# Attention's values with two products per head instead of four, and the two parts summed afterwards

## The chip, the core and the metric

The kernel runs on one core of a Trainium2 chip. The core's engines work side by side, each through its own list of instructions in order: TensorE (PE: matrix products, with PEld for its weight loads), VectorE (DVE), ScalarE (ACT), GpSimd (POOL) and SyncE (SP, which issues transfers). They wait for each other through semaphores. The metric is the device time of one execution in microseconds (us); the median of several timed executions is given.

## What is computed

One decoder layer with 256 positions, 1024 channels and 8 heads of 64. With 256 positions there is one block of keys, so the attention is plain causal attention. Cut to what matters here:

```python
proj  = x @ w_in                     # q, k, v, and the inputs of the convolution and of the gates
p     = softmax(causal(q @ k.T) * scale)
y_att = (p @ v) @ w_attn_out         # the change is in p @ v, head by head
y_cnv = (B * causal_dwconv3(C * h)) @ w_conv_out
mix   = (sigmoid(g_att) * y_att + sigmoid(g_cnv) * y_cnv) @ w_o
x     = layer_norm(alpha * x + mix)
u     = causal_dwconv3(x @ w_up)
x     = layer_norm(alpha * x + (silu(u_gate) * u_val) @ w_down)
```

## The kernel before

**Two parts.** Every float32 operand of a product is split into a high part h (rounded to the type float32r) and a low part l = x - h. A product is the sum of h·h, h·l and l·h. For weights ACT makes h (tile `wh`, L212) and DVE makes l (tile `wl`, L222) from what the transfer brought (tile `raw`).

**Stages.** The products with `w_in` come first: q, k, v, then h, c, b of the convolution, then sixteen column blocks of the gates, g0 to g15. After them come y0 to y7 (the products with `w_attn_out` and `w_conv_out`), `w_o`, and the feed-forward part. Attention and convolution are worked out beside the gate products: DVE and ACT do their elementwise work while PE is on g0 to g15.

**Order.** The order on each engine is written out by hand. Work goes in slots, one for each unit of weights. The table `STEPS` says at which half slot each piece is issued on its engine: entry s is the first or second half of slot s // 2. An engine keeps that order; a piece that waits holds up all that stands behind it on the same engine.

**Attention's values.** Heads go in pairs p = 0 to 3, with j = 0, 1 inside a pair. `vpt` holds the values (`vp`: for each head, 64 columns of high parts and 64 of low parts) and the transposed probabilities (`PT`: a = 0 the high part, a = 1 the low part, made by L501 on ACT and L241 on DVE). `attend` forms the products (tile `av`), placed behind the products of slots 13, 19, 22 and 24: behind g1, g7, g10 and g12. In a result the first 64 rows come from the high parts of the values, the other 64 from the low parts. `attend_out` lets ACT copy the lower rows out of the bank (tile `ac`), `attend_sum` lets DVE add the upper rows, and `attend_h` and `attend_l` split the sum into the tile `aT`, which y0 to y7 read.

**Banks.** PSUM has eight banks of 512 columns. In this stage four (`acc_bank`) go round among g0 to g3, g6, g7 and g10 to g15, so that g15 takes the bank of g11 and g14 that of g10. The other four (`ps_bank`) serve the scores, the values (`av`), and g4, g5, g8 and g9. A gate block leaves its bank through two instructions: ACT copies one half out (tile `gs`, L847), then DVE adds the other half (L856, into the tile `gates`). Only then can the next owner of the bank begin on PE.

Of the kernel before, what the change touches and what calls it, by code (L numbers as in the profile page):

```python
# [13 lines left out]
AF = mybir.ActivationFunctionType  # L14
ALU = mybir.AluOpType

P = 128
S = 256
# [3 lines left out]
HD = 64  # L22
# [122 lines left out]
def layer_kernel(ctx: ExitStack, tc: tile.TileContext, x, wpack, cpack, ln1_g, ln1_b, ln2_g, ln2_b, out):  # L145
    nc = tc.nc
# [13 lines left out]
    def ps_bank(name):  # L160
        return ps_pool.tile([P, 512], F32, tag="ps", name=name)

    def scratch(shape, name, bufs=None, tag="scr"):
        return tmp.tile(shape, F32, tag=tag, name=name, bufs=bufs or 6)
# [75 lines left out]
    def low(l, src, h):  # L240
        nc.vector.tensor_tensor(l, src, h.bitcast(F32), op=ALU.subtract)  # L241
# [133 lines left out]
    vp = vpt[:, 0:2048].rearrange("p (t g n) -> p t g n", t=2, g=4)  # L375
    PT = vpt[:, 2048:3584].rearrange("p (a j n) -> p a j n", a=2, j=2)
    aT = yT = None
# [50 lines left out]
    SB, SM, PR = {}, {}, {}  # L428
# [77 lines left out]
    def attend(p):  # L506


        o = PR[p, "o"] = ps_bank(f"av{p}").rearrange("p (j s) -> p j s", j=2)
        for j in range(2):  # L510
            js = slice(j * P, (j + 1) * P)
            for a in range(2):
                nc.tensor.matmul(o[:, j], vp[:, 0, p, js], PT[:, a, j, 0:256], start=a == 0, stop=False)
            for a in range(2):
                nc.tensor.matmul(o[:, j, P:S], vp[:, 1, p, js], PT[:, a, j, 256:384], start=False, stop=a == 1)

    def attend_out(p):

        c = PR[p, "c"] = scratch([P, 2, S], f"ac{p}")
        nc.scalar.activation(c[0:HD], PR[p, "o"][HD:P], AF.Copy)  # L520

    def attend_sum(p):
        c, o = PR[p, "c"], PR[p, "o"]
        nc.vector.tensor_tensor(c[HD:P, 0], o[0:HD, 1], c[0:HD, 1], op=ALU.add)
        nc.vector.tensor_tensor(c[0:HD, 0], o[0:HD, 0], c[0:HD, 0], op=ALU.add)

    def attend_h(p):
        nonlocal aT
        if aT is None:
            aT = big.tile([P, 4, 2, S], F32R, tag="d8", name="aT")  # L530
        nc.scalar.activation(aT[:, p, 0, :], PR[p, "c"][:, 0], AF.Copy)

    def attend_l(p):
        low(aT[:, p, 1, :], PR[p, "c"][:, 0], aT[:, p, 0, :])

# [48 lines left out]
    def open_ps():  # L586
# [10 lines left out]
             s=[5, 11],  # L597
# [5 lines left out]
             h=[24, 30, 38, 44],  # L603
             l=[25, 36, 39, 45],
             av=[13, 19, 22, 24],
             out=[26, 39, 44, 49],
             sum=[35, 42, 49, 51],
             ah=[41, 47, 50, 54],
             al=[44, 52, 53, 55],
             c1=[21, 35],  # L610
# [35 lines left out]
    for p in range(4):  # L646
        on(1, STEPS["m"][p], masked, p)
        on(0, STEPS["e"][p], exps, p)
        on(1, STEPS["n"][p], normalize, p)
        on(1, STEPS["n"][p], probs_halves, p)  # L650
        on(1, STEPS["n"][p], probs_T, p)
        on(STEPS["wE"][p], STEPS["w"][p], probs_words, p)
        on(0, STEPS["h"][p], probs_h, p)
        on(1, STEPS["l"][p], probs_l, p)
        at(C0 + STEPS["av"][p], "pe", attend, p)
        on(0, STEPS["out"][p], attend_out, p)
        on(1, STEPS["sum"][p], attend_sum, p)
        on(0, STEPS["ah"][p], attend_h, p)
        on(1, STEPS["al"][p], attend_l, p)
# [542 lines left out]
    for k, (kind, i, u) in enumerate(seq[:tail_from]):  # L1202
        if kind == "u":
            c, v = i
# [143 lines left out]
```

## Time and profile before

| | |
|---|---|
| median of 3 timed executions | 357.79 us (357.71 to 358.07) |
| span of the profiled execution, first to last instruction | 355.8 us |
| timed median less that span | 2.0 us |
| PE busy | 348.1 us (98% of the span) |
| DVE busy | 302.0 us (85%) |
| ACT busy | 243.8 us (69%) |
| GpSimd busy | 15.5 us (4%) |

A busy time is the sum of what the engine's instructions took, without their overlaps. Products are pipelined, so that the distance between two starts, not the length of one, is what a product costs PE. The shares are averages over stages that differ.

### The profile page before, as it was taken

To read this page: it belongs to the slowest core of one execution; us is meant where nothing else is said; L and a number is where in the kernel's file an instruction comes from. 1 tells how busy PE (TensorE), PEld (TensorE's weight loads), DVE (VectorE), ACT (ScalarE), POOL (GpSimd) and SP (SyncE) were. 2 spreads that over 40 slices of the span, in tenths; PEclk is the share of its full clock that TensorE was granted. 3 is DMA by queue.
4 is the path that set the end of the run, shared out by engine and by line. 5 is a ranking of instruction groups with operands and counts; after the bars stand their busy time and mean duration, and the time that the engine had idled before them with its cause. 6 is when DMAs were issued, how large, how long until landed. Compare 5 with 4: busy or idle time off the path is not lost.

```text
span 355.8 us, 4907 instructions
## 1 busy us (share of the span) xinstructions
PE 348.1 (98%) x1739; PEld 294.6 (83%) x1739; DVE 302.0 (85%) x521; ACT 243.8 (69%) x391; POOL 15.5 (4%) x41
## 2 busy tenths in 40 slices
PE   9999999999999999999999999999999999999992
PEld 8888888888988888888888888888888888888881
DVE  4787787997999989989668969997998786999975
ACT  3767857889998976652557487794968576578800
POOL 2000000000000012410000000000000000000120
PEclk9999999999999999999999999999999999999998
DMA  7995986887575685689187775889769693833003
GB/s 244 428 395 204 232 280 236 151 256 206 130 255 186 204 331 202 204 304 354 30 206 236 238 192 222 243 243 341 188 268 251 239 291 125 281 131 121 0 0 119
DMA packets 44904, 77.99 MB, mean 219 GB/s; under 512 B 34896, under 2 KB 35536, under 8 KB 37840
## 3 DMA queue, kind: packets, MB, share of 16 engines
q1 hardware_dynamic: 44304, 75.59, 65.9%
q0 software_dynamic: 576, 2.10, 2.0%
q8 instruction: 13, 0.21, 0.3%
q14 instruction: 11, 0.09, 0.1%
HBM read 68.24 MB, written 1.05 MB: 195 GB/s over the span
## 4 chain that ended last, share of the span: by engine, by line
PE 95%; issue 2%; DVE 1%; POOLq 0%; POOL 0%; DVEq 0%
PE g L351 8%; PE u L333 8%; PE u L335 8%; PE u L334 8%; PE qk L692 6%; PE d L335 5%; PE d L333 5%; PE d L334 5%; PE g L358 4%; PE y L351 4%; PE pb L351 4%; PE v L692 3%; PE pb L358 2%; PE y L358 2%; PE o L335 2%; PE o L334 2%
## 5 line engine op out<-in xcount | busy, mean ns | idle before, releaser
L222 DVE TENSOR_TENSOR wl<-raw,wh 128x1024 fp32r<-128x1024 f32 x99 | 119.8, 1223 | 15.5 <-ACT wh L212 15.4
L212 ACT ACTIVATE wh<-raw 128x1024 fp32r<-128x1024 f32 x99 | 101.8, 1054 | 8.6 <-DMA raw<-in_wpack 8.6
L333 PE MATMUL u<-wh,x1T 128*128 128x512 f32 x128 | 49.8, 389 | 0.0
L334 PE MATMUL u<-wl,x1T 128*128 128x512 f32 x128 | 49.8, 389 | 0.0
L335 PE MATMUL u<-wh,x1T 128*128 128x512 f32 x128 | 49.8, 389 | 0.0
L351 PE MATMUL g<-xT,wh 128*128 128x512 f32 x128 | 31.2, 393 | 0.0
L333 PE MATMUL d<-wh,f 128*128 128x512 f32 x76 | 29.6, 389 | 0.0
L334 PE MATMUL d<-wl,f 128*128 128x512 f32 x76 | 29.6, 389 | 0.0
L335 PE MATMUL d<-wh,f 128*128 128x512 f32 x76 | 29.6, 389 | 0.0
L245 DVE TENSOR_TENSOR wl<-raw,wh 128x1024 fp32r<-128x1024 f32 (+2 forms) x28 | 26.2, 982 | 3.4 <-ACT wh L244 3.3
L335 PEld LDWEIGHTS u<-wh,x1T 128*128 128x128 f32 x128 | 24.0, 188 | 5.0
L334 PEld LDWEIGHTS u<-wl,x1T 128*128 128x128 f32 x128 | 24.0, 188 | 5.0
L333 PEld LDWEIGHTS u<-wh,x1T 128*128 128x128 f32 x128 | 24.0, 188 | 4.9
L1035 ACT ACTIVATE fc<-pb,consts 128x256 f32<-128x256 f32 x36 | 16.4, 504 | 16.1 <-DVE pb L1077 16.1
L244 ACT ACTIVATE wh<-raw 128x1024 fp32r<-128x1024 f32 (+2 forms) x28 | 22.7, 860 | 6.8 <-PE o L335 4.0
L351 PEld LDWEIGHTS g<-xT,wh 128*128 128x128 f32 x128 | 23.3, 188 | 4.6
L1068 ACT ACTIVATE up<-u 128x1024 uint16<-128x1024 uint16 x16 | 15.5, 1018 | 9.7 <-PE u L335 6.9
L692 PE MATMUL qk<-wh,xT 128*128 128x512 f32 x60 | 19.2, 390 | 0.0
L1043 DVE SCALAR_TENSOR_TENSOR fc<-pb,consts,fc 128x254 f32<-128x254 f32 x36 | 17.4, 483 | 1.3
L1041 DVE SCALAR_TENSOR_TENSOR fc<-pb,consts,fc 128x255 f32<-128x255 f32 x36 | 17.2, 479 | 0.0
L358 PEld LDWEIGHTS g<-xT,wl 128*128 128x128 f32 x128 | 16.4, 191 | 0.6
L335 PEld LDWEIGHTS d<-wh,f 128*128 128x128 f32 x76 | 14.3, 188 | 3.0
(217 smaller groups left out, 684.2 us busy)
## 6 DMA issues: line engine op xcount, KB each, us to landing
raw<-in_wpack SPq DMA_DIRECT2D x55, 1024.0 KB, 5.2
raw<-in_wpack SPq DMA_DIRECT2D x6, 896.0 KB, 11.5
xr<-in_x SPq DMA_DIRECT2D x1, 1024.0 KB, 7.2
ln<-in_ln_g POOLq DMA_DIRECT2D x2, 512.0 KB, 5.6
ln<-in_ln_b POOLq DMA_DIRECT2D x2, 512.0 KB, 6.2
raw<-in_wpack SPq DMA_DIRECT2D x3, 256.0 KB, 3.9
raw<-in_wpack SPq DMA_DIRECT2D x1, 512.0 KB, 6.1
out<-x SPq DMA_DIRECT2D x1, 512.0 KB, 2.6
```

The lines of the kernel that those rows point to most:

```text
L212: nc.scalar.activation(units[u]["h"], raw_of(u), AF.Copy)
L222: nc.vector.tensor_tensor(units[u]["l"], raw_of(u), units[u]["h"].bitcast(F32), op=ALU.subtract)
L244: nc.scalar.activation(h, src, AF.Copy)
L245: (eng or nc.vector).tensor_tensor(l, src, h.bitcast(F32), op=ALU.subtract)
L333: nc.tensor.matmul(o, ah, bh, start=start, stop=False)
L334: nc.tensor.matmul(o, ah, bl, start=False, stop=False)
L335: nc.tensor.matmul(o, al, bh, start=False, stop=stop)
L351: nc.tensor.matmul(bank, un["h"][:, k, n0:n0 + P], b[:, k].rearrange("p a s -> p (a s)"), start=k == 0, stop=False)
L358: nc.tensor.matmul(bank[:, 0:S], un["l"][:, k, n0:n0 + P], b[:, k, 0], start=False, stop=k == nk - 1)
L692: nc.tensor.matmul(banks[m][t], (xl if p == 2 else xh)[:, k, t * P:(t + 1) * P], wl if p == 1 else wh, start=k == 0 and p == 0, stop=k == ...
L1041: nc.vector.scalar_tensor_tensor(c[:, 1:S], pb[:, a * S:a * S + S - 1], w_ffn(1, j), c[:, 1:S], op0=ALU.mult, op1=ALU.add)
L1043: nc.vector.scalar_tensor_tensor(c[:, 2:S], pb[:, a * S:a * S + S - 2], w_ffn(0, j), c[:, 2:S], op0=ALU.mult, op1=ALU.add)
```

## The change

Before, a head takes two products of 256 columns (one for each part of the probabilities) and two of 128 columns, all into one half of a bank: PE adds the two parts. Now a head takes one product of 512 columns, which holds both parts side by side, and one of 256; each head has a bank of its own, and the two parts stay side by side in it. So ACT copies two tiles per pair instead of one, DVE adds two 64x512 instead of two 64x256, and GpSimd adds the two parts at the end. Three entries of `out` and two of `sum` go one half slot earlier.

```diff
     def attend(p):
-        o = PR[p, "o"] = ps_bank(f"av{p}").rearrange("p (j s) -> p j s", j=2)
+        o = PR[p, "o"] = [ps_bank(f"av{p}_{j}").rearrange("p (a s) -> p a s", a=2) for j in range(2)]
         for j in range(2):
             js = slice(j * P, (j + 1) * P)
-            for a in range(2):
-                nc.tensor.matmul(o[:, j], vp[:, 0, p, js], PT[:, a, j, 0:256], start=a == 0, stop=False)
-            for a in range(2):
-                nc.tensor.matmul(o[:, j, P:S], vp[:, 1, p, js], PT[:, a, j, 256:384], start=False, stop=a == 1)
+            nc.tensor.matmul(o[j], vp[:, 0, p, js], PT[:, :, j, 0:256], start=True, stop=False)
+            nc.tensor.matmul(o[j][:, :, P:S], vp[:, 1, p, js], PT[:, :, j, 256:384], start=False, stop=True)
 
     def attend_out(p):
-        c = PR[p, "c"] = scratch([P, 2, S], f"ac{p}")
-        nc.scalar.activation(c[0:HD], PR[p, "o"][HD:P], AF.Copy)
+        PR[p, "c"] = [scratch([P, 2, S], f"ac{p}_{j}") for j in range(2)]
+        for j in range(2):
+            nc.scalar.activation(PR[p, "c"][j][0:HD], PR[p, "o"][j][HD:P], AF.Copy)
 
     def attend_sum(p):
         c, o = PR[p, "c"], PR[p, "o"]
-        nc.vector.tensor_tensor(c[HD:P, 0], o[0:HD, 1], c[0:HD, 1], op=ALU.add)
-        nc.vector.tensor_tensor(c[0:HD, 0], o[0:HD, 0], c[0:HD, 0], op=ALU.add)
+        for j in range(2):
+            nc.vector.tensor_tensor(c[0][j * HD:(j + 1) * HD], o[j][0:HD], c[j][0:HD], op=ALU.add)
+        nc.gpsimd.tensor_tensor(c[0][:, 0], c[0][:, 0], c[0][:, 1], op=ALU.add)
...
-             out=[26, 39, 44, 49],
-             sum=[35, 42, 49, 51],
+             out=[26, 38, 44, 48],
+             sum=[35, 42, 48, 50],
```

What this does to the order shows at three places. The first is DVE near the end of the gate blocks, before the change (names carry the number of their block or pair: `g11` is block 11, `ac2` the sum of pair 2):

```order
L856 TENSOR_TENSOR gates_916<-g9_1132,gs9_1228 128x256
L222 TENSOR_TENSOR wl51_1268<-raw21_1018,wh51_1192 128x1024
L222 TENSOR_TENSOR wl52_1270<-raw22_1100,wh52_1233 128x1024
L856 TENSOR_TENSOR gates_916<-g10_1168,gs10_1257 128x256
L524 TENSOR_TENSOR ac2_1188<-av2_1177,ac2_1188 64x256
L525 TENSOR_TENSOR ac2_1188<-av2_1177,ac2_1188 64x256
L815 TENSOR_TENSOR ct1_1097<-cb1_1013,ct1_1097 128x512
L222 TENSOR_TENSOR wl53_1306<-raw22_1100,wh53_1260 128x1024
L856 TENSOR_TENSOR gates_916<-g11_1203,gs11_1301 128x256
L524 TENSOR_TENSOR ac3_1266<-av3_1248,ac3_1266 64x256
L525 TENSOR_TENSOR ac3_1266<-av3_1248,ac3_1266 64x256
```

The same place now:

```order
L856 TENSOR_TENSOR gates_915<-g9_1131,gs9_1227 128x256
L524 TENSOR_TENSOR ac2_0_1185<-av2_0_1177,ac2_0_1185 64x512
L524 TENSOR_TENSOR ac2_0_1185<-av2_1_1178,ac2_1_1186 64x512
L222 TENSOR_TENSOR wl51_1269<-raw21_1017,wh51_1191 128x1024
L222 TENSOR_TENSOR wl52_1271<-raw22_1101,wh52_1232 128x1024
L856 TENSOR_TENSOR gates_915<-g10_1168,gs10_1253 128x256
L815 TENSOR_TENSOR ct1_1098<-cb1_1012,ct1_1098 128x512
L524 TENSOR_TENSOR ac3_0_1255<-av3_0_1247,ac3_0_1255 64x512
L524 TENSOR_TENSOR ac3_0_1255<-av3_1_1248,ac3_1_1256 64x512
L222 TENSOR_TENSOR wl53_1308<-raw22_1101,wh53_1260 128x1024
L856 TENSOR_TENSOR gates_915<-g11_1202,gs11_1300 128x256
```

The sums of pair 2 stand ahead of the low parts `wl51` and `wl52`, and those of pair 3 stand ahead of `wl53` and of the gate sum of g11, behind which they stood.

The second place is ACT around the copies of pair 1, before (`vpt` is the high part of pair 2's probabilities, which DVE's low part needs):

```order
L847 ACTIVATE gs5_1094<-g5_986 128x256
L501 ACTIVATE vpt_153<-sm23_824 128x768
L805 ACTIVATE ct1_1097<-z1_1028,consts_146 128x256
L859 ACTIVATE gates_916<-gates_916,consts_146 128x256
L212 ACTIVATE wh48_1102<-raw20_950 128x1024
L520 ACTIVATE ac1_1104<-av1_1085 64x512
```

and now:

```order
L847 ACTIVATE gs5_1091<-g5_985 128x256
L519 ACTIVATE ac1_0_1093<-av1_0_1085 64x512
L519 ACTIVATE ac1_1_1094<-av1_1_1086 64x512
L501 ACTIVATE vpt_153<-sm23_824 128x768
L805 ACTIVATE ct1_1098<-z1_1028,consts_146 128x256
L859 ACTIVATE gates_915<-gates_915,consts_146 128x256
L212 ACTIVATE wh48_1103<-raw20_949 128x1024
```

Two copies, each as large as the one before, now stand ahead of the probabilities' high part instead of one behind it.

The third place is GpSimd, whose list had nothing between its constants and the sums of the mix (L906); the piece of the difference:

```order
 L279 MEMSET invf 128x1 x8
+L525 TENSOR_TENSOR ac_0_893<-ac_0_893 128x256
+L525 TENSOR_TENSOR ac_0_1093<-ac_0_1093 128x256
+L525 TENSOR_TENSOR ac_0_1185<-ac_0_1185 128x256
+L525 TENSOR_TENSOR ac_0_1255<-ac_0_1255 128x256
 L906 TENSOR_TENSOR m_1420<-m_1420 128x256
```

There is one new sum of 128x256 per pair, released by the second of DVE's sums.

The banks of the `ps_bank` pool change hands too, since a pair takes two. Pair 1 now takes the banks of pair 0, g8 that of g4, g9 that of g5, pair 2 those of pair 1, and pair 3 those of g8 and g9. The four banks of `acc_bank` go round as before.

## Rows read from the trace of the kernel before

**Rows 1.** The page: PE's busy time, its granted clock, the chain that ended last

```profile
PE 348.1 (98%) x1739; PEld 294.6 (83%) x1739; DVE 302.0 (85%) x521; ACT 243.8 (69%) x391; POOL 15.5 (4%) x41
PEclk9999999999999999999999999999999999999998
PE 95%; issue 2%; DVE 1%; POOLq 0%; POOL 0%; DVEq 0%
```

**Rows 2.** Waits of PE over the whole span: us in total, times, longest

```profile
PE warm L258 <- PEq L1338: 0.8, 1, 0.8
```

**Rows 3.** Busy time by engine in two stretches of 10 us (columns: first line)

```profile
core 0: us, PE busy (x) PEld busy (x) DVE busy (x) ACT busy (x) POOL busy (x), PEclk, DMA share, GB/s
100.00:110.00 10.00, 10.00 (x64) 9.02 (x63) 9.80 (x16) 9.95 (x17) 0.00 (x0) 1.00 0.54 164
110.00:120.00 10.00, 10.00 (x59) 8.76 (x58) 9.54 (x16) 9.03 (x18) 0.00 (x0) 1.00 0.76 266
```

**Rows 4.** Timeline of PE around pairs 2 and 3: start us, us, engine, line, tiles

```profile
105.53 0.40 PE L513 MATMUL av<-vpt 128*128 128x256 f32 x2
...
106.40 2.05 PE L351 MATMUL g<-xT,wh 128*128 128x512 f32 x8
108.29 2.08 PE L358 MATMUL g<-xT,wl 128*128 128x256 f32 x16
110.20 2.00 PE L351 MATMUL g<-xT,wh 128*128 128x512 f32 x8
112.05 0.40 PE L513 MATMUL av<-vpt 128*128 128x256 f32 x2
...
116.72 3.82 PE L351 MATMUL g<-xT,wh 128*128 128x512 f32 x16
```

**Rows 5.** Timeline of DVE, g10's gate sum to pair 3's sums

```profile
113.83 0.42 DVE L856 TENSOR_TENSOR gates<-g,gs 128x256 f32<-128x256 f32 x1
114.28 0.42 DVE L524 TENSOR_TENSOR ac<-av,ac 64x256 f32<-64x256 f32 x1
114.71 0.42 DVE L525 TENSOR_TENSOR ac<-av,ac 64x256 f32<-64x256 f32 x1
115.05 0.67 DVE L815 TENSOR_TENSOR ct<-cb,ct 128x512 f32<-128x512 f32 x1
115.65 1.21 DVE L222 TENSOR_TENSOR wl<-raw,wh 128x1024 fp32r<-128x1024 f32 x1
117.23 0.42 DVE L856 TENSOR_TENSOR gates<-g,gs 128x256 f32<-128x256 f32 x1 [0.37 <-ACT gs L847]
117.69 0.42 DVE L524 TENSOR_TENSOR ac<-av,ac 64x256 f32<-64x256 f32 x1
```

**Rows 6.** DVE's sums of 512 columns out of a bank: ns min/median/max

```profile
L901 DVE TENSOR_TENSOR m<-y,m x8: 676/692/694, 125.9 to 145.5; 128x512 f32<-128x512 f32 x8
```

**Rows 7.** Timeline of ACT and DVE around pair 2's probabilities

```profile
98.45 0.37 ACT L847 ACTIVATE gs<-g 128x256 f32<-128x256 f32 x1
98.72 0.84 ACT L501 ACTIVATE vpt<-sm 128x768 fp32r<-128x768 f32 x1
99.20 0.42 DVE L856 TENSOR_TENSOR gates<-g,gs 128x256 f32<-128x256 f32 x1
99.59 0.96 DVE L241 TENSOR_TENSOR vpt<-sm,vpt 128x768 fp32r<-128x768 f32 x1
```

**Rows 8.** Timeline of ACT: one copy of a pair, and what follows

```profile
107.85 0.60 ACT L520 ACTIVATE ac<-av 64x512 f32<-64x512 f32 x1
108.35 0.83 ACT L501 ACTIVATE vpt<-sm 128x768 fp32r<-128x768 f32 x1
```

**Rows 9.** Timeline of DVE and GpSimd at the last sum of the mix

```profile
147.88 0.42 DVE L241 TENSOR_TENSOR mT<-m,mT 128x256 fp32r<-128x256 f32 x1
...
148.11 0.78 POOL L906 TENSOR_TENSOR m<-m 128x256 f32<-128x256 f32 x1 [0.79 <-DVE m L905]
148.21 1.76 DVE L222 TENSOR_TENSOR wl<-raw,wh 128x1024 fp32r<-128x1024 f32 x1
```

More of the change, by code (lines that the diff above doesn't have):

```diff
@@ L530, in attend_h @@
             aT = big.tile([P, 4, 2, S], F32R, tag="d8", name="aT")
-        nc.scalar.activation(aT[:, p, 0, :], PR[p, "c"][:, 0], AF.Copy)
+        nc.scalar.activation(aT[:, p, 0, :], PR[p, "c"][0][:, 0], AF.Copy)
     def attend_l(p):
-        low(aT[:, p, 1, :], PR[p, "c"][:, 0], aT[:, p, 0, :])
+        low(aT[:, p, 1, :], PR[p, "c"][0][:, 0], aT[:, p, 0, :])
     beside = {}
```

## The prediction

> **What bounds the kernel now.** I read the page first. PE is busy for 348.1 of 355.8 us, its granted clock is full in every slice until the last, and the chain that ended last is PE for 95% [rows 1]. The view of waits says the same more sharply: in the whole span PE waits once, for 0.8 us at the start [rows 2]. So time taken off PE's own work is time won, as long as PE still waits for nobody, and any wait that PE gets is time lost for good, because nothing behind it has slack to give back.
>
> Whether PE will wait is read from the stage of the change. Between 100 and 120 us DVE is busy for 9.80 and 9.54 of 10 us and ACT for 9.95 and 9.03 [rows 3]. These two are nearly as full as PE. In 20 us DVE is idle for 0.66 us. The change moves work from PE to DVE, ACT and GpSimd exactly there, so the sum needs both sides.
>
> **What PE saves.** A pair's eight products take from 105.53 to 106.40, 0.87 us [rows 4]. The prices of the new ones are in the neighbours: eight products of 512 columns take from 110.20 to 112.05, 0.231 us each, and sixteen of 256 columns from 108.29 to 110.20, 0.119 us each [rows 4]. A pair now needs two of each: 0.70 us. That saves 0.17 us per pair and 0.7 us in all four. No row shows a product whose 512 columns lie in two stretches; at worst it takes away the whole saving (0.87 again), at best it costs nothing. I take nothing, because the columns are as many as in the neighbours and each stretch is 256 long.
>
> **Where PE meets DVE.** The tightest place I find is g15. It takes the bank of g11, and may start when DVE's gate sum of g11 has ended. That sum runs from 117.23 to 117.65 [rows 5]. PE starts g14 at 116.72 and comes to g15 eight products later, at 116.72 + 8 × 0.231 = 118.57 [rows 4]. So the slack is 0.92 us, and with 0.7 us saved on PE it is 0.22 us. The question is how much later DVE ends that gate sum. Step by step:
>
> 1. *Longer sums.* A pair's two sums take from 114.28 to 115.05, 0.77 us, and the first of them starts 0.45 us after the gate sum before it, where L525 lets its follower start after 0.34 us (115.05 less 114.71); together 0.88 us [rows 5]. Now they are 64x512. The nearest rows are the sums of 512 columns out of a bank, 0.69 us [rows 6]; the one on SBUF lets its follower start after 0.60 us (115.05 to 115.65) [rows 5]. The two old sums started 0.43 us apart, a full length and not an overlapped one, so I take full lengths: 1.38 us, 0.50 more per pair. Lower end 1.20 (0.32 more), upper end 1.49 with the late start as well (0.61 more). Pairs 0, 1 and 2 stand ahead of g11's gate sum in both kernels: 1.5 us (0.96 to 1.83).
> 2. *Pair 3 moves ahead of it.* Its sums stood behind the gate sum of g11 and now stand ahead of `wl53` and of it: 1.38 us (1.20 to 1.49).
> 3. *A new wait for ACT.* Two copies of pair 1 now stand ahead of the high part of pair 2's probabilities. A copy lets its follower start after 0.50 us (107.85 to 108.35) [rows 8], so that L501 goes from 98.72 to 99.72 and ends at 100.56 [rows 7]. DVE, 0.5 us late from pair 0, would want it at 99.59 + 0.50 = 100.09 [rows 7]. It waits for 0.5 us (0.7 if a copy costs its full 0.60; 0 if the copies hide). What DVE loses on pair 0 beyond its longer sums is covered by this wait. Queued behind it are all of DVE's later pieces, so the delay stays.
> 4. *GpSimd beside DVE.* The trace has one encounter [rows 9]: a sum of two SBUF tiles (mT) runs on DVE, GpSimd's L906 begins at 148.11, and DVE's next low part starts at 148.21 and takes 1.76 us, where the same instruction takes 1.21 [rows 5]. It is 0.55 us longer. Each new sum on GpSimd has L906's size and starts right behind DVE's second sum. Behind pair 2 come `wl51` and `wl52`, both with two SBUF inputs, the same picture: 0.55 us. Behind pair 1 comes a gate sum that reads a bank, then `aT` with two SBUF inputs, which GpSimd, already 0.3 us on its way, holds up for some 0.4 us. Pair 0's falls under step 3's wait, pair 3's comes after g11's gate sum. Together 0.9 us (0 to 1.1).
> 5. *What absorbs.* Before its gate sum of g11 DVE idles for 0.37 us, waiting for ACT [rows 5]. A DVE that is late no longer does: 0.4 us off.
>
> The sum is 1.5 + 1.4 + 0.5 + 0.9 - 0.4 = 3.9 us. The gate sum of g11 ends at 117.65 + 3.9 = 121.55, and g15 starts then instead of at 118.57: 3.0 us later. PE will also wait for a bank at places before this, where banks of the smaller pool are handed on later than they were (g9 after g5's gate sum, pair 2 after pair 1's sums, pair 3 after g9's gate sum). These waits only use up the lead; they add nothing, because g15's start is set by DVE. The earlier entries of `out` and `sum` are in steps 2 and 3. Copies of pair 0 cost nothing that I count: each can start when its own head's products are done, and ACT has time there. Transfers are issued behind DVE's low parts, so some go out later, but PE's need for them moves by as much.
>
> There is a rule of the Trainium skill behind step 4, in "SBUF — State Buffer", section "Who interferes with whom": a DVE instruction with two SBUF inputs and a GpSimd instruction that reads SBUF share a read port, and the second to issue is blocked until the first is done. The trace agrees in the one encounter, with 1.76 against 1.21 us. By the rule the change ends 3.0 us late, and without it 2.1 us.
>
> The profiled execution's span is 355.8 us, and the median of the runs 357.79, so 2.0 us lie around the span. 355.8 + 3.0 = 358.8, and with 2.0 around it 360.8 us.
>
> **The rivals.** *GpSimd costs DVE nothing.* Step 4 rests on one row, and DVE's other sums beside L906 read a bank. Then the sum is 3.0, g15 starts 2.1 us late, and the time is 359.9 us. *Cheap sums.* If the new sums overlap as well as those on SBUF and ACT's copies hide, the lower ends give 0.96 + 1.20 - 0.4 = 1.8 on DVE, 0.8 us at g15, 358.6 us. *Dearer.* The upper ends give 1.83 + 1.49 + 0.7 + 1.1 - 0.4 = 4.7, 3.8 us at g15, 361.6 us.
>
> *The other side: the saving arrives whole.* PE is the bound [rows 1] and 0.7 us of its work goes away: 357.1 us. This decides if DVE ends the gate sum of g11 less than 0.22 us later than now. For it speaks that PE never waits today [rows 2]. Against it speaks that pair 3's sums alone put 1.2 us or more ahead of that gate sum, and that DVE has 0.66 us of idle time in 20 us to hide it in [rows 3]. Between 0.22 and 1.6 us on DVE the saving is eaten and no change can be measured. "Perfetto Trace Analysis" of the Trainium skill, section "Optimizing Tensor Performance", says that larger products are more efficient than smaller ones where they can be had; that rule is this rival's, and no more of it is seen in the trace than the 0.17 us per pair.
>
> *The change doesn't do what it says:* two stretches cost as much as two products. Then PE saves nothing, but since DVE sets g15's start the time stays at 360.8 us.
>
> **How the numbers follow.** A measurement of this kernel can tell 0.2% (0.72 us) from no change. The forecast with GpSimd's price has 0.50, without it 0.25, dearer 0.06, cheap sums 0.08 (half of it measurable), the saving eaten 0.05, the saving whole 0.06. As the whole saving of 0.7 us is just at what can be measured, half of that counts as faster. So slower has 0.85, the same 0.12, faster 0.03. The range goes from the cheap sums, 358.6, to just above the dearer case, 361.8 us.
>
> **What would show it.** In the changed kernel PE should have waits on DVE's L856 at a gate block, the longest at the sixteenth (L351 `g`, over 1 us). Step 1 is right if L524 takes 0.69 us; step 3 if DVE waits for ACT's `vpt`; step 4 if a low part behind pair 2's sums takes 1.7 us. PE's block of a pair should last 0.70 us where it does not wait. The prediction is wrong if PE shows no wait between 95 and 125 us, if y0 starts before its old time, or if something later in the kernel, where PE had no wait before, gives the delay back.

## The result, and the profile after

The changed kernel takes 360.9 us (median of 4, 360.38 to 361.06) where the kernel before takes 357.75 beside it (4 executions). The ratio is 1.0082, with a 95% interval of 1.007 to 1.0094. It is slower by 3.15 us; 360.8 was forecast.

The page of the kernel after: busy times, PE's granted clock, the chain that ended last.

```profile
PE 348.8 (97%) x1723; PEld 293.3 (82%) x1723; DVE 305.3 (85%) x521; ACT 245.7 (68%) x395; POOL 20.8 (6%) x45
PEclk9999999999999999999999999999999999999999
PE 75%; ACT 9%; DVE 7%; DMA 4%; issue 3%; SPq 1%; POOLq 0%; POOL 0%; DVEq 0%; ACTq 0%
```

Against [rows 1] the clock is as full as it was, so the difference is not PE's speed. PE has 16 products fewer, and yet its share of the chain falls from 95% to 75%: DVE and ACT now stand on it. The waits of PE say where (us in total, times, longest).

```profile
PE g L351 <- DVE gates L856: 2.4, 2, 1.5
PE warm L258 <- PEq L1338: 0.8, 1, 0.8
PE av L512 <- DVE gates L856: 0.5, 1, 0.5
```

Before there was only the wait of 0.8 us at the start [rows 2]. Now the view lists three waits of PE for a gate sum of DVE, that is for a bank. The stage in two stretches of 10 us (columns as in [rows 3]):

```profile
100.00:110.00 10.00, 9.11 (x51) 7.69 (x50) 9.74 (x16) 9.96 (x18) 0.74 (x1) 1.00 0.67 221
110.00:120.00 10.00, 9.35 (x55) 7.95 (x54) 9.92 (x14) 9.28 (x17) 1.71 (x1) 1.00 0.50 181
```

PE was busy for all of both stretches and now is for 9.11 and 9.35 us; DVE, already at 9.80 and 9.54, stands at 9.74 and 9.92. The timeline of PE shows the three places, with pair 0's block ahead of them and the start of y0 behind them (it answers to [rows 4]).

```profile
80.18 0.40 PE L512 MATMUL av<-vpt 128*128 128x512 f32 x1
...
80.89 3.80 PE L351 MATMUL g<-xT,wh 128*128 128x512 f32 x16
...
101.16 2.11 PE L351 MATMUL g<-xT,wh 128*128 128x512 f32 x8 [0.89 <-DVE gates L856]
...
114.18 0.47 PE L512 MATMUL av<-vpt 128*128 128x512 f32 x1 [0.50 <-DVE gates L856]
...
116.43 2.07 PE L358 MATMUL g<-xT,wl 128*128 128x256 f32 x16
118.65 2.11 PE L351 MATMUL g<-xT,wh 128*128 128x512 f32 x8
122.25 2.06 PE L351 MATMUL g<-xT,wh 128*128 128x512 f32 x8 [1.48 <-DVE gates L856]
...
126.06 1.09 PE L351 MATMUL y<-yT,wh 128*128 128x512 f32 x4
```

The waits are at g9 (101.16), at the second bank of pair 3 (114.18) and, longest, at g15 (122.25). Pair 0's block takes 0.71 us (80.18 to 80.89). What a wait costs PE is the gap between starts, which is more than the figure in brackets, since that counts from the modelled end of the product before. At g15: the product due at 118.65 + 8 × 0.231 = 120.50 begins at 122.25, 1.75 us late where the bracket says 1.48. By this measure there is a fourth, short wait without a bracket: g14 was due at 116.43 + 16 × 0.119 = 118.33 and begins at 118.65, behind the gate sum of g10 whose bank it takes (DVE's trace has that sum from 118.19 to 118.60). So a short wait can stand in no view of waits. DVE over the same stretch (it answers to [rows 5]):

```profile
113.96 1.37 DVE L524 TENSOR_TENSOR ac<-av,ac 64x512 f32<-64x512 f32 x2
115.36 2.91 DVE L222 TENSOR_TENSOR wl<-raw,wh 128x1024 fp32r<-128x1024 f32 x2
...
119.12 1.39 DVE L524 TENSOR_TENSOR ac<-av,ac 64x512 f32<-64x512 f32 x2
120.54 1.23 DVE L222 TENSOR_TENSOR wl<-raw,wh 128x1024 fp32r<-128x1024 f32 x1
121.68 0.42 DVE L856 TENSOR_TENSOR gates<-g,gs 128x256 f32<-128x256 f32 x1
122.02 0.61 DVE L241 TENSOR_TENSOR aT<-ac,aT 128x256 fp32r<-128x256 f32 x1
```

The row at 121.68 is the gate sum of g11, which ended at 117.65 before [rows 5] and ends at 122.10 now; g15 begins 0.15 us behind it. Between the start of pair 3's sums and that gate sum DVE has no gap: 119.12, 120.54, 121.68.

The profiled execution after reaches pair 0's products at 80.18, before at 79.57, though nothing is changed ahead of them; these 0.61 us are variation between executions (in the runs below it is 79.13 to 80.74). So all comparisons of traces below go by the time from the start of pair 0's products to the start of y0. Before, the two rows and the one behind pair 0 are:

```profile
79.57 0.40 PE L513 MATMUL av<-vpt 128*128 128x256 f32 x2
...
80.45 3.87 PE L351 MATMUL g<-xT,wh 128*128 128x512 f32 x16
...
122.28 1.09 PE L351 MATMUL y<-yT,wh 128*128 128x512 f32 x4
```

That is 42.71 us before and 126.06 - 80.18 = 45.88 after, 3.17 us longer. The timed difference is 3.15 us, as much as this stretch is longer. Behind y0 the span is 0.4 us shorter after the change than before (233.1 us against 233.5), no more than the runs below differ there among themselves (233.1 to 234.0).

### The profile page after: what moved, and what is told of

Same layout as the page of the kernel before. It is cut to its first block, busy times and chain, and to the rows that moved or that the text cites. A ratio compares the mean times of both kernels' runs of the same rounds, so it can differ in the third digit from the quotient of the medians.

```text
span 359.2 us, 4884 instructions
## 1 busy us (share of the span) xinstructions
PE 348.8 (97%) x1723; PEld 293.3 (82%) x1723; DVE 305.3 (85%) x521; ACT 245.7 (68%) x395; POOL 20.8 (6%) x45
## 4 chain that ended last, share of the span: by engine, by line
PE 75%; ACT 9%; DVE 7%; DMA 4%; issue 3%; SPq 1%; POOLq 0%; POOL 0%; DVEq 0%; ACTq 0%
PE u L334 8%; PE u L333 8%; PE u L335 8%; PE d L334 5%; PE d L333 5%; PE d L335 5%; PE qk L692 5%; PE y L351 4%; PE pb L351 4%; ACT wh L212 3%; DVE wl L222 2%; DMA raw<-in_wpack 2%; PE v L692 2%; PE pb L358 2%; PE y L358 2%
```

## The experiments

The theory: PE's saving is real, but DVE, with no room left, frees banks later, because its sums are longer, because pair 3's stand ahead of g11's gate sum, and because GpSimd's sums hold DVE up. The rivals are four: GpSimd costs nothing; the order alone is the cause; the handing-on of banks costs by itself, whatever DVE does; the new products are no cheaper.

All runs in one table: the time, the ratio to the kernel before on the same chip with its interval, the starts of pair 0's products and of y0 in the trace, and how much longer the stretch between them is than 42.71 us.

| run | us (executions) | ratio | pair 0, y0 | longer by |
|---|---|---|---|---|
| the change | 360.9 (4) | 1.0082, 1.007 to 1.0094 | 80.18, 126.06 | 3.17 |
| e1_no_pool | 360.12 (5) | 1.0063, 1.005 to 1.0076 | 79.77, 124.75 | 2.27 |
| e2_order_back | 359.75 (5) | 1.0059, 1.0045 to 1.0073 | 79.91, 124.09 | 1.47 |
| e3_order_back_no_pool | 358.31 (11) | 1.0013, 1.0005 to 1.0022 | 79.85, 122.81 | 0.25 |
| e4_one_part | 356.98 (11) | 0.998, 0.9972 to 0.9989 | 79.76, 121.59 | -0.88 |
| e5_steps_alone | 357.89 (11) | 0.9999, 0.9991 to 1.0008 | 79.13, 121.99 | 0.15 |
| e6_add_on_vector | 361.37 (5) | 1.0104, 1.0088 to 1.0121 | 80.10, 126.06 | 3.25 |
| e7_other_banks | 360.62 (6) | 1.0071, 1.0055 to 1.0087 | 79.50, 124.54 | 2.33 |
| e8_retuned | 359.35 (5) | 1.0038, 1.0026 to 1.005 | 80.61, 124.25 | 0.93 |
| e9_back_on_vector | 359.43 (6) | 1.0042, 1.003 to 1.0054 | 80.01, 123.76 | 1.04 |
| e10_two_pairs | 357.97 (12) | 1.001, 0.9997 to 1.0022 | 80.74, 124.68 | 1.23 |
| e11_two_pairs_again | 357.53 (11) | 0.9989, 0.998 to 0.9998 | 79.81, 122.13 | -0.39 |

The kernel before took 357.84 us beside e1 to e4, 357.95 beside e5 to e8, 357.8 beside e9 and e10, and 357.9 beside e11. The last column ends at the start of y0. In e2, e8 and e9 PE waits for DVE once more in the y products behind that (0.3 to 0.4 us), so that their time is longer by more than the column says.

### e1: without GpSimd's sums

```diff
-        nc.gpsimd.tensor_tensor(c[0][:, 0], c[0][:, 0], c[0][:, 1], op=ALU.add)
```

> The changed kernel without GpSimd's four sums; it leaves out that the upper 256 columns of each pair's result (the products with the low parts of the probabilities) are added. Theory (DVE sets g15's start, and GpSimd's sums hold DVE up by 0.56 us behind pair 2 and 0.4 us behind pair 1): the two low parts behind pair 2's sums take 2.35 us again instead of 2.91, aT 0.41 instead of 0.80, the gate sum of g11 ends 0.95 us sooner, PE's wait at g15 falls from 1.48 to some 0.5 us, and the time is 359.9 us. Rival (GpSimd costs DVE nothing, the long pair of low parts has another cause): 360.9 us, as with them.

Timelines of GpSimd (all four sums), DVE and ACT in the changed kernel (ACT's row is the high part of pair 2's probabilities, for which DVE's row at 101.23 waits):

```profile
93.88 1.23 POOL L525 TENSOR_TENSOR ac<-ac 128x256 f32<-128x256 f32 x1 [91.19 <-DVE ac L524]
107.16 0.74 POOL L525 TENSOR_TENSOR ac<-ac 128x256 f32<-128x256 f32 x1 [12.05 <-DVE ac L524]
115.47 1.71 POOL L525 TENSOR_TENSOR ac<-ac 128x256 f32<-128x256 f32 x1 [7.57 <-DVE ac L524]
120.59 1.76 POOL L525 TENSOR_TENSOR ac<-ac 128x256 f32<-128x256 f32 x1 [3.41 <-DVE ac L524]
...
94.45 1.29 DVE L783 COPY z<-z 128x1024 uint16<-128x1024 uint16 x1
...
101.23 0.96 DVE L241 TENSOR_TENSOR vpt<-sm,vpt 128x768 fp32r<-128x768 f32 x1
...
107.39 0.80 DVE L241 TENSOR_TENSOR aT<-ac,aT 128x256 fp32r<-128x256 f32 x1
...
100.36 0.83 ACT L501 ACTIVATE vpt<-sm 128x768 fp32r<-128x768 f32 x1
```

The same pieces of DVE in e1, with the low parts behind pair 2's sums and DVE's wait for ACT:

```profile
94.04 0.76 DVE L783 COPY z<-z 128x1024 uint16<-128x1024 uint16 x1
100.84 0.96 DVE L241 TENSOR_TENSOR vpt<-sm,vpt 128x768 fp32r<-128x768 f32 x1 [0.68 <-ACT vpt L501]
106.99 0.42 DVE L241 TENSOR_TENSOR aT<-ac,aT 128x256 fp32r<-128x256 f32 x1
114.58 2.36 DVE L222 TENSOR_TENSOR wl<-raw,wh 128x1024 fp32r<-128x1024 f32 x2
```

Waits of PE in e1, but the one at the start:

```profile
PE g L351 <- DVE gates L856: 1.7, 2, 1.3
```

With GpSimd's sums the copy (L783) takes 1.29 us instead of 0.76, aT 0.80 instead of 0.42, the two low parts 2.91 instead of 2.36. The last two make 0.93 us, and y0 comes 0.90 us sooner without them. The copy's 0.53 us were covered: without them DVE waits for ACT instead, 0.68 us, and begins the low part of pair 2's probabilities as late as with them (21.07 and 21.05 us after pair 0's products). The rival that GpSimd costs nothing falls. Where the gain shows was expected wrongly: the wait at g15 falls only from 1.48 to 1.33 us and not to 0.5, and most of the gain comes at g9 (0.35 us instead of 0.89) and at pair 3 (none listed instead of 0.50). A PE that waits less on the way comes sooner to g15 and waits there for most of what it won. GpSimd pays as well: its sum takes 0.74 us by itself and 1.71 where it meets a low part that has begun. There the first low part keeps its length and the second is the long one, 1.76 us. The Trainium skill, "SBUF — State Buffer", section "Who interferes with whom", has DVE and GpSimd share a pair of ports as an exclusive lock; a DVE piece with two SBUF inputs contends for it with a GpSimd instruction that reads SBUF, and a copy does in some of its modes. The trace agrees for the first with 0.38 and 0.55 us, and the copy's 0.53 us fit, though no run shows in which mode it ran.

### e2 and e3: the order of the kernel before, with and without GpSimd's sums

```diff
-             out=[26, 38, 44, 48],
-             sum=[35, 42, 48, 50],
+             out=[26, 39, 44, 49],
+             sum=[35, 42, 49, 51],
```

e3 has the edit of e1 as well.

> The changed kernel with the entries of out and sum of the kernel before. Theory (step 2, pair 3's sums ahead of g11's gate sum, is 1.4 us of g15's delay): the gate sum of g11 ends 1.4 us sooner, and 0.2 us more because DVE no longer waits for ACT at pair 2's probabilities; PE's 1.48 us at g15 go, and what is left are the bank waits ahead of it: 359.3 us (359.0 to 360.1, the upper end if the adds of GpSimd, which then start beside other sums of DVE, hold those up for another 0.5 us or so). Rival (the order doesn't matter, only the length of the work): DVE has the same work in front of the end of the stage, so 360.7 us or more.

> Both edits: order of the kernel before and no sums on GpSimd; it leaves out the same addition. Theory (both act on the same sum of DVE): the gate sum of g11 ends 2.5 us sooner than in the changed kernel, PE does not wait for it, and only the longer sums of step 1 are left, which PE meets at the earlier bank hand-overs: 358.5 us (358.2 to 358.9). Rival (the delay is in the banks: a pair holds two, and g9, pair 3 and g14 get theirs late whatever DVE does later): PE keeps the 1.7 us that it waits ahead of g15 in the changed kernel, less 0.7 us saved, so 1.0 us late: 358.8 us or more, and the waits at g9 and at the second bank of pair 3 stand as they are (0.89 and 0.50 us).

Timelines of GpSimd, DVE and PE in e2:

```profile
117.58 1.18 POOL L525 TENSOR_TENSOR ac<-ac 128x256 f32<-128x256 f32 x1 [10.17 <-DVE ac L524]
...
118.07 1.77 DVE L222 TENSOR_TENSOR wl<-raw,wh 128x1024 fp32r<-128x1024 f32 x1
...
120.23 2.12 PE L351 MATMUL g<-xT,wh 128*128 128x512 f32 x8 [0.37 <-DVE gates L856]
125.03 0.70 PE L351 MATMUL y<-yT,wh 128*128 128x512 f32 x2 [0.31 <-DVE yT L241]
```

y0 begins 1.70 us sooner than with the change and then waits 0.31 us in its middle, which leaves 1.39 (1.24 by the clock: 3.15 above the kernel before against 1.91). The wait at g15 falls from 1.48 to 0.37 us. It does not go altogether, and the time is in the upper part of the expected range, for the reason given there: pair 2's sum on GpSimd now runs at 117.58, and `wl53` behind it takes 1.77 us instead of 1.23.

Without GpSimd's sums hardly anything is left to wait for at g15 (0.1 us by the distance between starts). Waits of PE in e3 from pair 0 on:

```profile
PE g L351 <- DVE gates L856: 0.3, 1, 0.3
PE av L512 <- DVE gates L856: 0.2, 1, 0.2
```

358.31 us against 358.5 expected. The waits at g9 and at pair 3 shrink from 0.89 and 0.50 to 0.33 and 0.19 us, though each pair still holds two banks. So the banks were late because DVE was, and the rival that they cost by themselves falls; e4, with the same banks and no wait at all, confirms it. The two causes don't simply add up: the old order is worth 1.39 us at y0 with GpSimd's sums and 2.02 without them (e1 to e3), and GpSimd's sums cost 0.90 us in the changed order and 1.53 in the old one (the wait in the middle of y0 counted with it).

### e4: PE's side alone

```diff
-            nc.scalar.activation(PR[p, "c"][j][0:HD], PR[p, "o"][j][HD:P], AF.Copy)
+            nc.scalar.activation(PR[p, "c"][j][0:HD, 0], PR[p, "o"][j][HD:P, 0], AF.Copy)
...
-            nc.vector.tensor_tensor(c[0][j * HD:(j + 1) * HD], o[j][0:HD], c[j][0:HD], op=ALU.add)
-        nc.gpsimd.tensor_tensor(c[0][:, 0], c[0][:, 0], c[0][:, 1], op=ALU.add)
+            nc.vector.tensor_tensor(c[0][j * HD:(j + 1) * HD, 0], o[j][0:HD, 0], c[j][0:HD, 0], op=ALU.add)
```

It has the order of e2 too.

> PE's side of the change alone: the products and banks as changed, the order of the kernel before, ACT copies and DVE adds only the first 256 columns of each bank (as many columns in all as before, in twice as many instructions on ACT), no sums on GpSimd; it leaves out the products with the low parts of the probabilities in the sum. Theory (all lost time comes from the extra elementwise work on DVE): PE's block of a pair takes 0.70 us, 0.7 us are saved, and PE waits at most for what the bank hand-overs take of them: 357.1 us (357.0 to 357.7). Rival (two banks per pair cost by themselves: g9 and pair 3 wait for banks that were free before): 358.2 us or more, with PE waiting over 1 us for gate sums. Rival (two stretches cost as much as two products): blocks of 0.87 us, 357.8 us without a wait of PE.

Waits of PE in e4, all of them:

```profile
PE warm L258 <- PEq L1338: 0.8, 1, 0.8
```

With the same products in the same banks, and as many columns on ACT and DVE as before, PE waits for nothing and the kernel is faster than the one before: 356.98 us, at the lower edge of what was expected, y0 0.88 us sooner. That is 0.22 us per pair. The block of pair 0 itself is 0.71 us instead of 0.88 (79.76 to 80.47 in e4, the same length as in the change); of the rest a part stands in the sixteen products behind it, 3.80 us instead of 3.87, again as in the change. The new products are cheaper, and what took this back is elementwise work and where it stands.

### e5: the order alone

> The kernel before with the changed entries of out and sum and nothing else: pair 3's sums of two times 64x256 move ahead of g11's gate sum, and one copy instead of two moves ahead of the probabilities' high part. Theory (there are 0.92 us of slack at g15, and the change is dear because the moved sums are long): the moved sums cost DVE 0.88 us, the copy some 0.2 us, 0.37 us of idle time absorb a part, so the gate sum of g11 ends 0.7 us later and PE doesn't wait: 357.8 us, no change. Rival (the moved entries are the cause by themselves): a PE wait at g15 and 358.5 us or more.

Its edit is the lines `out` and `sum` of the change in the kernel before; two entries differ in each, not three in `out` as was said with the change. The time is the same, and the view of waits has nothing for PE but the 0.8 us at the start. The new wait of DVE for ACT can be seen by itself in DVE's timeline, and behind it g11's gate sum:

```profile
99.73 0.96 DVE L241 TENSOR_TENSOR vpt<-sm,vpt 128x768 fp32r<-128x768 f32 x1 [0.59 <-ACT vpt L501]
...
117.60 0.41 DVE L856 TENSOR_TENSOR gates<-g,gs 128x256 f32<-128x256 f32 x1
```

Counted from pair 0's products the gate sum ends 0.80 us later than before, and the 0.15 us by which y0 is later arise in g14 and g15, whose first sixteen products take 3.80 us instead of 3.65. So the moved entries use up about the whole slack of 0.92 us, and hardly more: moving pair 3's sums ahead of g11's gate sum is all but free while they are short and nothing else is late. In the changed kernel the slack that paid for it was already spent.

### e6 and e9: the last sum on DVE

```diff
-        nc.gpsimd.tensor_tensor(c[0][:, 0], c[0][:, 0], c[0][:, 1], op=ALU.add)
+        nc.vector.tensor_tensor(c[0][:, 0], c[0][:, 0], c[0][:, 1], op=ALU.add)
```

e9 has the order of e2 as well.

> The changed kernel with the last sum of a pair on DVE instead of GpSimd. Theory (GpSimd's sum of 0.74 us holds DVE up by about as much as DVE would need for it): the 0.95 us of holding up fall away, and three sums of 128x256 of 0.34 us from start to start come in ahead of g11's gate sum (pair 0's lies under the wait for ACT, which was 0.68 us without GpSimd's sums): 360.8 us (360.6 to 361.1), the same as on GpSimd within 0.3 us. Rival (GpSimd takes the work off DVE for nothing): four times 0.34 us more than the changed kernel: 362.2 us.

> The changed kernel with the entries of out and sum of the kernel before and the last sum of each pair on DVE. Everything is computed. Theory (what counts is how much DVE has to do ahead of a hand-over): against the run with this order and no last sum, which was 0.5 us above the kernel before, three sums of 0.34 us come in ahead of g11's gate sum, 1.0 us: 359.4 us (359.1 to 359.6), no worse than the same order with the sum on GpSimd (1.9 us above the kernel before). Rival (GpSimd is the cheaper place after all, as the timed runs of the two on the changed order hint, by 0.5 us): 360.3 us.

Timeline of DVE in e6, behind pair 2's sums:

```profile
115.23 0.42 DVE L525 TENSOR_TENSOR ac<-ac 128x256 f32<-128x256 f32 x1
115.58 2.35 DVE L222 TENSOR_TENSOR wl<-raw,wh 128x1024 fp32r<-128x1024 f32 x2
```

DVE needs 0.35 us for the sum (115.23 to 115.58) and gets 0.56 us back on the two low parts. In the trace e6 is 0.08 us behind the change. By the clock it is 361.37 us, 0.3 above the upper end expected and 0.5 above the change, though the intervals of the two ratios overlap. With the order of before, DVE is no worse a place than GpSimd: 359.43 as expected, beside 359.75 with GpSimd, where again the intervals overlap. Which place is better is not shown. In neither order does GpSimd relieve DVE by what the rival says, 1.36 us.

### e7 and e8: other banks, another order

e7 changes one entry of the changed kernel, the gate blocks that take banks of the smaller pool:

```diff
-             ps=(4, 8),
+             ps=(4, 10),
```

e8 has it too, and

```diff
-             out=[26, 38, 44, 48],
-             sum=[35, 42, 48, 50],
+             out=[26, 38, 45, 48],
+             sum=[37, 44, 46, 50],
...
-             al=[44, 52, 53, 55],
+             al=[44, 54, 53, 55],
```

with seven other entries in `lal`, the table that places the low parts of the weights.

> The changed kernel with g10 and g11 in the smaller pool of banks and g8 and g9 in the larger one, so that g15 no longer takes the bank of g11 but that of g9, which is free long before, and pair 3 takes the banks of pair 2. Order on DVE as changed. Theory (DVE is late with everything in this stage, so PE waits at whichever bank is handed on latest): no wait at g15, but pair 3 has to wait until pair 2's sums end, at 115.3 by the changed kernel's clock, where PE could begin at 112.7: some 2.4 us late in all instead of 3.2: 360.2 us (359.9 to 360.5), the wait now on L524. Rival (the hand-over from g11 to g15 is the one place that costs): PE gets the 1.48 us of g15 back and has only the smaller waits ahead of it: 359.4 us or less.

> The changed kernel with another order: sums and copies of pairs 1 to 3 moved so that none stands ahead of a gate sum that PE waits for soon, low parts put in at other places, and the banks as in the run before. Everything is computed. Theory (lateness at hand-overs is a matter of where DVE's extra 0.53 us per pair and the holding up by GpSimd are put; they can be spread but not removed): the wait at g15 goes and smaller waits of 0.3 to 0.8 us are left at pair 2, g11 and in the y products: 359.0 us (358.5 to 359.6), faster than the changed kernel, slower than the one before. Rival (the order was the whole cause): the 0.7 us of PE arrive, 357.1 us.

Waits of PE in e7, the longest:

```profile
PE av L512 <- DVE ac L524: 2.1, 2, 1.8
```

In e8 from pair 0 on:

```profile
PE av L512 <- DVE ac L524: 1.0, 1, 1.0
PE y L351 <- DVE m L901: 0.4, 1, 0.4
```

In e7 the wait at g15 is gone and one of 1.8 us stands at pair 3 in its place, for pair 2's sums. y0 is 2.33 us late where 2.4 was expected, 0.84 sooner than with the change; by the clock it is 360.62, 0.1 above the expected range, and the intervals of the two ratios overlap (the profiled execution, 359.50, is the fastest of the six). The hand-over from g11 to g15 was where DVE's lateness came out, not its cause. e8 spreads the waits and gets back about half, 359.35 us. No order that was run makes the whole change as fast as the kernel before.

### e10 and e11: two pairs of four

What e3 to e5 say together is that DVE has room for some of the new sums. Pairs 0 and 3 are formed in the new way, their last sum on DVE, in the kernel before:

```diff
+    WIDE = (0,3)
+
     def attend(p):
...
+        if p in WIDE:
...
-             sum=[35, 42, 49, 51],
+             sum=[35, 42, 49, 52],
...
-             al=[44, 52, 53, 55],
+             al=[44, 50, 53, 55],
```

> The kernel before with only pairs 0 and 3 formed with 512-column products, a bank per head, the two parts summed on DVE; pair 3's sums and the low part of pair 1's result placed a half slot or two elsewhere. Everything is computed. Theory (DVE has some room, which two pairs fill and four overrun): PE saves twice 0.22 us (the run with PE's side alone had y0 0.88 us sooner with four pairs); pair 0 puts 0.53 + 0.34 = 0.87 us on DVE ahead of g11's gate sum, of which 0.37 us of idle time absorb a part, and the slack of 0.92 us at g15, less the 0.44 us saved, takes the other 0.50; pair 3's come behind that gate sum: no PE wait of more than 0.1 us, and 357.5 us (357.2 to 357.8) beside 357.9 for the kernel before. Rival (any work added to DVE in this stage comes out on the path): 358.4 us or more, with a wait at g15 or at y0.

> The same kernel as in the run before, since its profiled execution was one in which a weight transfer landed late (ACT waited 2.43 us for it, and by that PE 1.36 us at g15), so that its trace doesn't show whether DVE has room for two pairs. Theory (it has): in an execution without that wait PE doesn't wait at g15, y0 begins 42.3 us after pair 0's products (42.7 in the kernel before), and the time is 357.5 us beside 357.8. Rival (the late transfer belongs to this order): the wait of ACT for the transfer and PE's at g15 are there again, and the time is 358.0 us or more.

The profiled execution of e10 took 360.18 us, the others between 357.26 and 358.41. Timelines of ACT, DVE and PE in it:

```profile
117.73 1.06 ACT L212 ACTIVATE wh<-raw 128x1024 fp32r<-128x1024 f32 x1 [2.43 <-DMA raw<-in_wpack]
...
120.33 0.42 DVE L874 TENSOR_TENSOR gates<-g,gs 128x256 f32<-128x256 f32 x1 [1.53 <-ACT gs L865]
...
120.81 2.11 PE L351 MATMUL g<-xT,wh 128*128 128x512 f32 x8 [1.36 <-DVE gates L874]
```

The lines are numbered otherwise in this kernel: L874 and L865 are the gate sum and its copy (L856 and L847 above), L538 the sums of 64x512. One weight transfer landed late; ACT waited for it, DVE's gate sum for ACT, and g15 for the gate sum. In e11, the same kernel, the only wait of PE is that at the start, and y0 comes 42.32 us after pair 0's products, as expected. DVE's timeline there:

```profile
117.80 0.41 DVE L874 TENSOR_TENSOR gates<-g,gs 128x256 f32<-128x256 f32 x1
118.14 1.39 DVE L538 TENSOR_TENSOR ac<-av,ac 64x512 f32<-64x512 f32 x2
```

Pair 3's sums now stand behind the gate sum. The gate sum of g11 ends at 118.21, in time for g15, if barely. So DVE has room for two pairs in the trace. By the clock this version is 357.97 and 357.53 us in two measurements; the interval of the first ratio holds 1, that of the second ends just below it (0.9998). Taken together that is no difference from the kernel before that can be told, and e10's own expectation was missed by 0.2 us.

## Why the prediction was right, point by point

**What PE saves.** 0.70 us per block was predicted, 0.71 measured; two stretches of 256 columns cost no more than one of 512. The term was under-sized all the same: 0.22 us per pair and not 0.17, since the products next to the block run closer too (e4). It did not move the forecast, because in the changed kernel DVE sets g15's start.

**Step 1, longer sums.** 0.50 us more per pair predicted. The sums take 671 to 685 ns, one pair's from 113.96 to 115.36, 1.40 us where it was 0.88: 0.52 more.

```profile
L524 DVE TENSOR_TENSOR ac<-av,ac x8: 671/680/685, 92.4 to 119.8; 64x512 f32<-64x512 f32 x8
```

On the path, e3 less e4 gives what the longer sums and copies of four pairs cost by themselves: 1.13 us at y0, 1.33 by the clock.

**Step 2, pair 3 ahead of the gate sum.** 1.38 us predicted; 119.12 to 120.54 is 1.42. The old order gives back 1.39 (e2), but that so close a match is partly luck: e2 also undoes step 3 and lets GpSimd hold up `wl53`, and without GpSimd's sums the same edit is worth 2.02. e5 adds what the prediction did not say: with the old sums the same move costs nothing by the clock.

**Step 3, the wait for ACT.** 0.5 us was predicted together with the claim that what DVE loses on pair 0 is covered by it. In the changed kernel the copy behind pair 0's sums took 0.53 us longer, and hardly any wait was left, some 0.2 us (the gate sum ahead starts at 100.69 and lets its follower start 0.34 us later); but DVE still begins right behind ACT (101.19 and 101.23), at 100.62 without the 0.61 us of the earlier stage, where 100.56 was predicted. Without GpSimd's sums the wait is 0.68 (e1). Each covers the other, as the step had it.

**Step 4, GpSimd.** 0.9 us predicted from one encounter; 0.38 and 0.55 measured, and 0.90 at y0 when the sums are left out (e1). This was the least certain term, with one row behind it, and the experiment shows it rather than argues it. The picture behind it was not quite right. Behind pair 2 it had GpSimd first and the next low part held; in the trace that low part is first, GpSimd waits for it, and the second low part is held, by the same amount. It also had pair 3's sum begin behind g11's gate sum. It begins ahead of it, at 120.59, beside `wl53`, and what it holds up is `aT` at 122.02 (0.61 us, 0.42 in e1), behind the gate sum: nothing is added at g15, as the sum had it.

**Step 5, absorbed idle time.** DVE's gap of 0.37 us ahead of g11's gate sum is gone.

**The sum.** g11's gate sum ends at 122.10, or 121.49 without the 0.61 us of the earlier stage, where 121.55 was predicted. The forecast let g15 start with the end of that sum; in the trace it starts 0.15 us behind it, at 121.64 counted in the same way. y0 comes 3.17 us late, where 3.0 was predicted for g15. PE's waits at g9 and pair 3 were called harmless as long as DVE sets g15's start, and in the changed kernel that holds. In e7, where g15 has another bank, a wait of that kind is the one that counts.

**The rivals.** The saving arrives whole when the added elementwise work is taken away and the order is the old one (e4), which is what that rival needed. Had GpSimd been free, 359.9 was predicted, and e1 took 360.12.

## What to carry to other kernels

Work that is taken off the bounding engine and given to a second one is won only as far as that one has idle time ahead of the next hand-over; here a change that takes 0.88 us off PE put a gate sum of DVE 3.8 us later, where DVE had 0.66 us free in 20. Read the slack at the place where the bounding engine next takes a buffer from the other, and add up all that is put ahead of it there, order and contention included. Here another bank moved such a wait, another order made it smaller, and only less work ahead of it, as with two pairs instead of four, made it go.

## What was not expected of the hardware

- GpSimd's sum of 128x256 holds up a copy on DVE with one input as well (uint16, 0.76 us in e1, e3 and e9, 1.29 in the change, e2 and e7), not only sums with two inputs in SBUF.
- A GpSimd sum that meets a low part running on DVE waits for its end and then holds up the piece behind it, in the change a second low part. 0.74 us of GpSimd's time became 1.71, and DVE still lost 0.55: two engines pay for one meeting. Behind pair 3 a gate sum, which reads a bank, stands there and was not held up (121.68, 0.42 us); `aT` behind it was.
- With the products of 128 columns gone, the sixteen of 512 behind pair 0 take 3.80 us instead of 3.87. Why is not shown.
